# The end of a hybrid block written in another order, with shorter inverse roots and rare transfers on another queue

## Chip, cores and metric

One core of a Trainium2 chip runs the whole program. The metric is the time of one execution on the device in microseconds, less is better; the time given is the median of the runs. Beside it there is one profiled execution, whose trace all times of single instructions come from.

## The reference

512 tokens of 1024 features go through two layers, all in float32.

```python
def first_block(x, ...):
    h = rms_norm(x, norm_mix_w)
    z, xbc, dt_raw, q, k, v, f_raw = split(h @ w_in)
    y_ssd = ssd_mixer(...)          # chunked scan, group norm
    y_fox = fox_mixer(...)          # attention with forget gates, norms of q and k per head
    x = x + concat(y_ssd, y_fox) @ w_out
    return x + conv_gated_mlp(rms_norm(x, norm_ffn_w), ...)

def second_block(x, p, ...):
    h = rms_norm_2(x, mix_norm_g)
    y_r = (silu(rg) * head_group_norm(retention_chunkwise(...))) @ w_ret_o
    y_s = sliding_window_gqa(...) @ w_swa_o
    x = x + (sigmoid(gate_r) * y_r + sigmoid(gate_s) * y_s) @ w_out
    x = x + hierarchical_moe(rms_norm_2(x, ffn_norm_g), ...)   # 32 experts, two for each token
    ple = rms_norm_2(p @ w_ple, ple_norm_g)
    return x + sigmoid(rms_norm_2(x, ple_gate_norm_g) @ w_ple_gate) * ple
```

Each norm holds `lax.rsqrt(mean(x * x) + eps)`.

## The kernel before, in words

Tokens lie in four blocks of 128 (`NT = 4`); a product that has to be as exact as float32 is made of three matmuls of high and low halves (`mm3`, L251 to L253), whose halves ScalarE (L205, high) and VectorE (L208, low) make.

**Inverse roots.** No engine instruction gives the root itself: `rsqrt` computes it on VectorE from a shifted integer as first guess and three Newton steps, ten rows of 128 x 1, or thirteen where several columns are done at once (L326 to L343). It is called 43 times, in the norms of both mixers, of the feed-forward parts and of the gate. Outside the experts the order on each engine is found by a scheduler from its own costs, so that fewer rows in one place can change the order of others.

**The experts.** Of 256 slots for four experts each (64 a piece), one-hot matmuls gather the tokens. Experts are worked off in pairs, e = 0, 2, ... 30, by the class `Pair`: it asks SyncE's queue for eight chunks of `wgu` and four of `wdn`, 512 KB each, into a ring of chunk tiles `wc`; `up` makes 32 matmuls (L1116) and the gated value `hid` (L1119, L1120); `turn` transposes it into `hT` (L354, L1128); `down` makes 16 matmuls (L1136) and copies the two sums into the row tile `ye` (L1138 on ScalarE, L1139 on VectorE). A pair up to e = 28 is scattered to the buffer `ydram` by an indirect transfer of GpSimd (L1531). After e = 28, eight indirect transfers of GpSimd (L1773) gather, for each token block, its rows of the two chosen experts into `hf` tiles. The last pair (e = 30) doesn't go that way: `turned` (at e = 28) builds its one-hots `ohw` with VectorE (L1541, L1542), TensorE transposes them, and VectorE makes the 0/1 matrix `late` and the slots' weights `wslot` from them (L1545 to L1547); in the tail the last rows, weighted and split in high and low halves (L1564, L1565), are added to the tokens by matmuls with `late` (`pair`, L1573).

**The tail** is the gate. For each block t, `gathered` adds the gathered rows to x[t] (L1583 on VectorE, or L1580 on ScalarE with L1581 on GpSimd), `end` adds the sum of the last pair (L1589), `turn` transposes and splits x[t], and `logits` multiplies it with the gate's weights, 24 matmuls for 512 columns. The weights come in eight chunks, four for each half of the columns; `split` makes their high halves on ScalarE (L1818) and their low ones on VectorE (L1819). `eat` (L1835 to L1838) does the sigmoid, the product with `ple`, the sum with x and the output transfer. The order of the calls in `tail` is written by hand and is the order of the rows on TensorE, ScalarE, VectorE and GpSimd.

**The overflow.** Behind the tail stands a loop that takes care of experts with over 64 tokens (`overflow`). It goes round zero times with these inputs, but its instructions are in every engine's program.

Of the kernel before, what the change touches and what calls it, by code (L numbers as in the profile page):

```python
# [19 lines left out]
T = 512  # L20
# [152 lines left out]
class Chip:  # L173
# [146 lines left out]
    def rsqrt(self, ss, scale, tag="rs", pool=None, more=None):  # L320
# [24 lines left out]

    def row(self, key, pool, tag="row", t=None):
# [3 lines left out]
        self.nc.sync.dma_start(t, self.a["rows"][:, o:o + n].to_broadcast([128, n]))  # L350
        return t
# [743 lines left out]
class Pair:  # L1095
# [4 lines left out]
    def __init__(self, c, p, rows, chunks, wgu, wdn):  # L1100
        self.c, self.p, self.n = c, p, len(wgu)
        fetch = lambda ws, i: [chunks.fetch(w[:, i * 1024:i * 1024 + 1024]) for w in ws]
# [26 lines left out]

    def down(self):  # L1130
        c, r = self.c, 64 * self.n
        ps = [c.acc() for _ in range(2)]
        for j in range(2):
            for n in range(2):
                for i in range(self.n):
                    c.nc.tensor.matmul(ps[n][self.half(i)], self.hT[:, j, self.half(i)],  # L1136
                                       self.wd[j][i][:, n * 512:n * 512 + 512], start=j == 0, stop=j == 1)
# [5 lines left out]
def overflow(c, x, routing, slot, wt, extra, pled, out):  # L1143

    tc, nc, a = c.tc, c.nc, c.a
    v, s, pe = nc.vector, nc.scalar, nc.tensor
# [5 lines left out]
    with tc.For_i(0, some, 1):  # L1152
# [5 lines left out]
        w = c.row("n_ffn2", p)  # L1158
# [10 lines left out]
        for t in range(NT):  # L1169
            nc.sync.dma_start(ple[:, t], pled[t])  # L1170
# [5 lines left out]
        for n in range(2):  # L1176
            w = [gate_weights(c, c.fetch(a["wpleg"][n][:, i * 1024:i * 1024 + 1024]), i) for i in range(4)]
            for t in range(NT):
# [4 lines left out]
                gated(c, g, ps, r[t], x[t][:, ns], ple[:, t, ns], out[t * 128:t * 128 + 128, ns])  # L1183
# [4 lines left out]
def more_rounds(c, p, ring, x, hf, rel, wt, iota, wgu, wdn, rounds):  # L1188
# [5 lines left out]
    with tc.For_i(0, rounds * N_EXP * SLOTS, N_EXP * SLOTS) as r:  # L1194
        with tc.For_i(0, N_EXP, 1) as e:
# [23 lines left out]
            ex = Pair(c, p, p, chunks, [wgu[rows]], [wdn[rows]])  # L1219
# [229 lines left out]
def experts(c, x, routing, xtp, pled, out):  # L1449
# [84 lines left out]
    def turned(oT, w):  # L1534

        s4 = slots4(7)
        sums = p.tile([128, NT], F32, name="wsum")
        for t in range(NT):
            o = [p.tile([128, 128], F32, name=c.name("ohw"), tag=tag, bufs=1) for tag in ("ohw", "ohw2")]
            for k in range(2):  # L1540
                v.tensor_scalar(o[k], iota[:, 128:], s4[:, k, t:t + 1], wt[:, k, t:t + 1], op0=OP.is_equal, op1=OP.mult)  # L1541
            v.tensor_tensor(o[0], o[0], o[1], op=OP.add)  # L1542
            ps = c.aux()
            c.transpose(ps[:, :128], o[0])
            v.tensor_scalar(oT[:, t * 128:t * 128 + 128], ps[:, :128], 0.0, None, op0=OP.is_gt)  # L1545
            v.tensor_reduce(sums[:, t:t + 1], ps[:, :128], axis=AX.X, op=OP.add)
        v.tensor_reduce(w, sums, axis=AX.X, op=OP.add)  # L1547

    def tail():

        y = last.rows
        xt = BlockTiles(c, moe)
        junk = op.tile([128, D], F32, name="junk", tag="ohq", bufs=1)
        raws, w, pairs, r = [], [], {}, {}

        def fetch(i):
            raws.append(chunks.fetch(a["wpleg"][i // 4][:, i % 4 * 1024:i % 4 * 1024 + 1024], nc.sync if i < 4 else nc.scalar))

        def split(i):
            w.append(gate_weights(c, raws[i], i, [chunks.tile(F32R) for _ in "hl"]))  # L1560

        def half(n):
            ns = slice(n * 512, n * 512 + 512)
            s.activation(yh[:, ns], y[:, ns], AF.Copy, scale=ws)  # L1564
            v.scalar_tensor_tensor(yl[:, ns], y[:, ns], ws, yh[:, ns].bitcast(F32), op0=OP.mult, op1=OP.subtract)  # L1565

        def pair(t):

            pairs[t] = []
            for n in range(2):  # L1570
                ps = c.aux()
# [4 lines left out]
        def gathered(t, k, on_pool):  # L1576

            yk, wk = yg[t][:, k], first[:, k, t:t + 1]
            if on_pool:
                s.activation(yk, yk, AF.Copy, scale=wk)  # L1580
                nc.gpsimd.tensor_tensor(x[t], x[t], yk, op=OP.add)  # L1581
            else:
                v.scalar_tensor_tensor(x[t], yk, wk, x[t], op0=OP.mult, op1=OP.add)  # L1583
# [9 lines left out]

        def squares(ts):
            ss = c.sm([128, len(ts)], tag="gss")
            for i, t in enumerate(ts):
                s.activation(junk, x[t], AF.Square, accum_out=ss[:, i:i + 1])
            rs = c.rsqrt(ss, 1.0 / D, "gr")
            r.update({t: rs[:, i:i + 1] for i, t in enumerate(ts)})

        def logits(t, n, between=lambda: None):
            ps = c.aux() if n else c.acc()
            gate(c, ps, xt(t), w[4 * n:4 * n + 4], between)
            return ps

        def eat(ps, t, o, n=512, eng=None):
# [302 lines left out]
```

## Time and profile before

| | |
|---|---|
| median of 3 runs | 1619.01 us (1618.94 to 1623.02) |
| profiled execution | 1617.72 us, its span 1616.0 us |
| TensorE busy | 1517.5 us (94%) |
| VectorE busy | 923.9 us (57%) |
| ScalarE busy | 667.4 us (41%) |
| GpSimd busy | 135.2 us (8%) |
| moved | 246.64 MB, 153 GB/s over the span |

The span is the time from the first to the last instruction in the trace; what lies around it (1.7 us) belongs to the execution's time. In the rows, PE is TensorE, PEld its weight loads, DVE VectorE, ACT ScalarE, POOL GpSimd, SP SyncE; a q behind the name is that engine's queue of transfers. L12 is line 12 of the kernel before.

### The profile page before, as it was taken

What the parts mean: (1) busy time and instruction counts of PE and PEld (TensorE: products, weight loads), DVE (VectorE), ACT (ScalarE), POOL (GpSimd) and SP (SyncE); (2) the same over time, 40 slices, a digit from 0 to 9 for tenths busy, and PEclk for the clock granted to TensorE, in tenths of its full rate; (3) what the DMA queues carried; (4) which work ended last, traced back from release to release, by engine and by line L of the source; (5) the groups of instructions that cost most, each with busy time, mean ns of one, the idle gap of its engine ahead of it and who ended that gap; (6) DMA issues with size and microseconds to landing.
All of it is one profiled execution on the core that took longest, in us unless ns stands there. A gap on an engine that the chain in (4) does not pass through costs nothing.

```text
span 1616.0 us, 24407 instructions
## 1 busy us (share of the span) xinstructions
PE 1517.5 (94%) x9603; PEld 1256.3 (78%) x9603; DVE 923.9 (57%) x2122; ACT 667.4 (41%) x1107; POOL 135.2 (8%) x114
## 2 busy tenths in 40 slices
PE   3998989999999999999999998899999999999867
PEld 3776888999899988998889997887889855545356
DVE  4368688888864765436544524877644552232274
ACT  3364637656742544224432323369622421111143
POOL 3043310000000000000000001200000010000142
PEclk9999999999999999999999999999999999999979
DMA  9242212222250533233323522221213889999951
GB/s 320 90 156 92 79 61 71 79 92 68 90 159 25 183 92 97 75 116 97 96 72 102 192 83 91 105 75 58 91 64 125 302 330 411 409 410 409 383 199 55
DMA packets 75946, 246.64 MB, mean 153 GB/s; under 512 B 9486, under 2 KB 18446, under 8 KB 75456
## 3 DMA queue, kind: packets, MB, share of 16 engines
q1 hardware_dynamic: 69152, 220.80, 38.9%
q0 software_dynamic: 4944, 17.91, 3.0%
q10 hardware_dynamic: 1728, 6.29, 1.0%
q8 instruction: 78, 1.28, 0.3%
q14 instruction: 44, 0.36, 0.1%
HBM read 234.86 MB, written 24.18 MB: 160 GB/s over the span
## 4 chain that ended last, share of the span: by engine, by line
PE 73%; DVE 14%; ACT 6%; issue 3%; DMA 2%; POOL 1%; SPq 0%; ACTq 0%; POOLq 0%; DVEq 0%
PE acc L251 17%; PE acc L252 17%; PE acc L253 17%; PE acc L1116 6%; PE acc L1136 3%; PE aux L1476 3%; PE aux L354 3%; DVE wl L208 2%; PE aux L634 1%; ACT wh L205 1%; DMA wr<-in_wz_dram 1%; DVE de L554 1%; ACT pb L611 1%; DVE xn L362 1%; DVE rst L338 1%
## 5 line engine op out<-in xcount | busy, mean ns | idle before, releaser
L208 DVE TENSOR_TENSOR wl<-wr,wh 128x1024 fp32r<-128x1024 f32 (+1 forms) x177 | 213.6, 1209 | 253.5 <-ACT wh L205 248.6
L205 ACT ACTIVATE wh<-wr 128x1024 fp32r<-128x1024 f32 (+1 forms) x181 | 188.6, 1046 | 319.7 <-PE acc L253 158.9
L252 PE MATMUL acc<-xtl,wh 128*128 128x512 f32 (+2 forms) x744 | 278.6, 375 | 0.0
L251 PE MATMUL acc<-xth,wh 128*128 128x512 f32 (+2 forms) x744 | 277.3, 373 | 1.3 <-ACT wh L205 1.2
L253 PE MATMUL acc<-xth,wl 128*128 128x512 f32 (+2 forms) x744 | 277.0, 372 | 0.0
L251 PE MATMUL acc<-wh,xth 128*128 128x256 f32 x912 | 257.8, 284 | 3.8 <-ACT xth L205 2.0
L253 PE MATMUL acc<-wh,xtl 128*128 128x256 f32 x912 | 258.4, 284 | 0.8 <-DVE xtl L208 0.8
L252 PE MATMUL acc<-wl,xth 128*128 128x256 f32 x912 | 257.3, 283 | 1.2 <-DVE wl L208 1.1
L251 PEld LDWEIGHTS acc<-wh,xth 128*128 128x128 f32 x912 | 172.8, 190 | 7.5 <-ACT z L415 3.6
L252 PEld LDWEIGHTS acc<-wl,xth 128*128 128x128 f32 x912 | 173.0, 190 | 2.5 <-DVE wl L208 1.8
L253 PEld LDWEIGHTS acc<-wh,xtl 128*128 128x128 f32 x912 | 172.8, 190 | 1.6 <-DVE xtl L208 1.0
L251 PEld LDWEIGHTS acc<-xth,wh 128*128 128x128 f32 (+1 forms) x744 | 139.4, 187 | 27.1 <-ACT wh L205 1.9
L253 PEld LDWEIGHTS acc<-xth,wl 128*128 128x128 f32 (+1 forms) x744 | 139.3, 187 | 25.1 <-issue 0.5
L252 PEld LDWEIGHTS acc<-xtl,wh 128*128 128x128 f32 (+1 forms) x744 | 139.3, 187 | 24.3 <-issue 0.5
L1116 PE MATMUL acc<-wc,xg 128*64 128x512 f32 x512 | 112.6, 592 | 0.0
L251 PE MATMUL acc<-wh,acth 128*128 128x256 f32 x352 | 98.7, 280 | 0.1
L253 PE MATMUL acc<-wh,actl 128*128 128x256 f32 x352 | 98.3, 280 | 0.0
L252 PE MATMUL acc<-wl,acth 128*128 128x256 f32 x352 | 98.2, 279 | 0.0
L1116 PEld LDWEIGHTS acc<-wc,xg 128*64 128x64 f32 x512 | 36.7, 137 | 72.8 <-issue 64.3
L251 PEld LDWEIGHTS acc<-wh,acth 128*128 128x128 f32 x352 | 66.5, 189 | 0.6 <-ACT acth L205 0.5
L773 DVE SCALAR_TENSOR_TENSOR fcv<-acc,cols,fcv 128x511 f32<-128x511 f32 x88 | 65.7, 747 | 1.6
L252 PEld LDWEIGHTS acc<-wl,acth 128*128 128x128 f32 x352 | 66.5, 189 | 0.1
(476 smaller groups left out, 2618.2 us busy)
## 6 DMA issues: line engine op xcount, KB each, us to landing
wc<-in_wgu_dram SPq DMA_DIRECT2D x128, 512.0 KB, 10.7
wc<-in_wdn_dram SPq DMA_DIRECT2D x64, 512.0 KB, 10.8
wr<-in_wup_dram SPq DMA_DIRECT2D x44, 512.0 KB, 3.6
wr<-in_w2a_dram SPq DMA_DIRECT2D x28, 512.0 KB, 3.6
wr<-in_wqkv_dram SPq DMA_DIRECT2D x24, 512.0 KB, 3.7
wr<-in_wout_dram SPq DMA_DIRECT2D x24, 512.0 KB, 3.8
wr<-in_wdown_dram SPq DMA_DIRECT2D x16, 512.0 KB, 3.5
ydram<-in_x_dram POOLq DMA_DIRECT2D x15, 512.0 KB, 9.9
```

Source lines behind the costliest of these rows:

```text
L205: nc.scalar.activation(hi, src, AF.Copy)
L208: (nc.vector if engines[1] == "v" else nc.gpsimd).tensor_tensor(lo, src, hi.bitcast(F32), op=OP.subtract)
L251: mm(out, a[0], b[0], start=start, stop=False)
L252: mm(out, a[0], b[1], start=False, stop=False)
L253: mm(out, a[1], b[0], start=False, stop=stop)
L338: v.scalar_tensor_tensor(t, y, y, ms, op0=OP.mult, op1=OP.mult)
L354: self.nc.tensor.transpose(out, src, self.ident[:rows, :rows])
L362: nc.vector.scalar_tensor_tensor(out, xt_, r, wrow, op0=OP.mult, op1=OP.mult)
L773: v.scalar_tensor_tensor(y[:, sh:], ps[:, :T - sh], cv(k), y[:, sh:], op0=OP.mult, op1=OP.add)
L1116: c.nc.tensor.matmul(ps[self.half(i)], xg(kb, i), self.wu[kb // 2][i][:, kb % 2 * 512:kb % 2 * 512 + 512], start=kb == 0, stop=kb == KB - 1)
L1136: c.nc.tensor.matmul(ps[n][self.half(i)], self.hT[:, j, self.half(i)], self.wd[j][i][:, n * 512:n * 512 + 512], start=j == 0, stop=j == 1)
L1476: pe.matmul(ps[:, j], hf[t][:, k, ks], oq[:, t], start=start and k == 0, stop=stop and k == 1)
```

## The change

It has four parts, and line numbers move.

- `rsqrt`: a first guess that takes the shift into the multiplication, and two steps instead of three, seven rows for one column and nine for several.
- The last pair's one-hots: `weighted` builds them for all blocks at e = 24, `turned` transposes them in one PSUM tile behind pair 28's down product, one row each for `late` and `wslot`.
- The tail in another order. The first four gate chunks are asked for when the last pair's own chunks are; the last pair's sums are read in PSUM (no copy into `ye`); all of `gathered` is on VectorE; the high and low halves of the weights are separate calls; block 0's product isn't interrupted by block 1's transposes; the products with `ple` are on VectorE.
- The overflow loop's transfers are asked for by GpSimd rather than SyncE.

Line numbers: L354 is L355, L1116 is L1117, L1136 is L1137, L1545 and L1546 are L1558 and L1559, L1565 is L1587, L1573 is L1595, L1583 is L1600, L1589 is L1606, L1819 is L1580 in the tail.

```diff
@@ rsqrt
-        v.tensor_scalar(t.bitcast(I32), ms.bitcast(I32), 1, None, op0=OP.logical_shift_right)
-        v.tensor_scalar(y.bitcast(I32), t.bitcast(I32), -1.0, float(0x5F3759DF), op0=OP.mult, op1=OP.add)
-        for k in (1.0, -2.0, 16.0):
+        v.tensor_scalar(y.bitcast(I32), ms.bitcast(I32), -0.5, -553040512.0, op0=OP.mult, op1=OP.add)
+        for step in range(2):
...
-            v.scalar_tensor_tensor(y, t, -3.0 * k * k, y, op0=OP.add, op1=OP.mult)
-        v.tensor_scalar(y, y, -1.0 / 8192, None, op0=OP.mult)
+            if step == 0:
+                v.scalar_tensor_tensor(t, t, -2.0539012, t, op0=OP.add, op1=OP.mult)
+            v.scalar_tensor_tensor(y, t, -1.8898816 if step else 1.8970146, y, op0=OP.add, op1=OP.mult)
@@ overflow
+    queue = nc.gpsimd
...
-            nc.sync.dma_start(xi, routing.xd[t * 128:t * 128 + 128])
+            queue.dma_start(xi, routing.xd[t * 128:t * 128 + 128])
@@ last one-hots
+    def weighted():
         s4 = slots4(7)
+        ow, o2 = (p.tile([128, n, 128], F32, name=name) for name, n in (("ohw", NT), ("ohw2", 1)))
         for t in range(NT):
+            for k, o in enumerate((ow[:, t], o2[:, 0])):
+                v.tensor_scalar(o, iota[:, 128:], s4[:, k, t:t + 1], wt[:, k, t:t + 1], op0=OP.is_equal, op1=OP.mult)
+            v.tensor_tensor(ow[:, t], ow[:, t], o2[:, 0], op=OP.add)
+        return ow
+    def turned(ow, oT, w):
+        ps = c.aux()
+        for t in range(NT):
+            c.transpose(ps[:, t * 128:t * 128 + 128], ow[:, t])
+        v.tensor_scalar(oT, ps, 0.0, None, op0=OP.is_gt)
+        v.tensor_reduce(w, ps, axis=AX.X, op=OP.add)
@@ tail
+        last.turn()
+        high(0)
+        low(0)
+        rows = last.products(True)
+        half(0, rows[0])
+        gathered(0, 0)
+        half(1, rows[1])
+        gathered(0, 1)
+        high(1)
+        pair(0)
+        pair(1)
+        end(0)
+        turn(0)
+        pair(2)
+        low(1)
+        for i in (2, 3):
+            high(i)
+            low(i)
+        ps = {0: logits(0, 0)}
+        block(1)
+        pair(3)
...
+        ps[1] = logits(1, 0, (6,), lambda: block(2))
+        ss = [squares((0, 1))]
+        ps[2] = logits(2, 0, (4,), lambda: block(3))
@@ loop over the pairs
+            if e + 2 == N_EXP:
+                raws = [fetch_gate(i) for i in range(4)]
...
+            if e == 24:
+                ow = weighted()
             if e < COMBINED:
                 last.turn()
...
+            if e == 28:
+                turned(ow, late[:, :T], ws)
```

`block(t)` is `gathered` twice, `end` and `turn`; `(6,)` and `(4,)` are the feature blocks of the eight ahead of which it is called.

**TensorE at pair 28.** The first fence is the order before, from the last matmul of the pair's up product to the down product (`wc` are the chunks, `ohw` the one-hots):

```order
L1116 MATMUL acc_14583<-wc_14572,xg_14351 64x512
L354 MATMUL aux_14615<-cst,ohw_14610 128x128
L354 MATMUL aux_14624<-cst,ohw_14619 128x128
L354 MATMUL aux_14633<-cst,ohw_14628 128x128
L354 MATMUL aux_14642<-cst,ohw_14637 128x128
L354 MATMUL aux_14647<-cst,hid_14600 128x128 x2
L1136 MATMUL acc_14652<-wc_14574,hT_14650 64x512
L1136 MATMUL acc_14652<-wc_14576,hT_14650 64x512
```

The second is the order after, the same place up to pair 30's up product:

```order
L1117 MATMUL acc_14461<-wc_14450,xg_14213 64x512
L355 MATMUL aux_14485<-cst,hid_14478 128x128 x2
L1137 MATMUL acc_14490<-wc_14452,hT_14488 64x512
...
L1137 MATMUL acc_14491<-wc_14458,hT_14488 64x512
L355 MATMUL aux_14505<-cst,ohw 128x128 x4
L1117 MATMUL acc_14573<-wc_14540,xg_14213 64x512
```

The one-hots' four transposes stood ahead of the transposes of `hid` and the down product; they now stand behind the down product, in one row.

**VectorE in the tail.** Before, from the first addition of a gathered row (`hf`) to x0 on; `wc` with `cols` is a row pair that makes the low half of a weight chunk:

```order
L1583 SCALAR_TENSOR_TENSOR x_1814_12069<-hf_14667,first,x_1814_12069 128x1024
L1819 SCALAR_TENSOR_TENSOR wc_14787<-wc_14746,cols,wc_14786 128x512 x2
L1583 SCALAR_TENSOR_TENSOR x_1814_12069<-hf_14667,first,x_1814_12069 128x1024
L1589 TENSOR_TENSOR x_1814_12069<-x_1814_12069,aux_14779 128x512
L1589 TENSOR_TENSOR x_1814_12069<-x_1814_12069,aux_14782 128x512
L1819 SCALAR_TENSOR_TENSOR wc_14798<-wc_14748,cols,wc_14797 128x512 x2
L208 TENSOR_TENSOR hf_14811<-aux_14812,hf_14811 128x512
L208 TENSOR_TENSOR hf_14811<-aux_14819,hf_14811 128x512
L1819 SCALAR_TENSOR_TENSOR wc_14827<-wc_14750,cols,wc_14826 128x512 x2
L1583 SCALAR_TENSOR_TENSOR x_1815_12070<-hf_14668,first,x_1815_12070 128x1024
L1589 TENSOR_TENSOR x_1815_12070<-x_1815_12070,aux_14805 128x512
```

After, from the low half of the first weight chunk on:

```order
L1580 SCALAR_TENSOR_TENSOR wc_14598<-wc_14565,cols,wc_14597 128x512 x2
L1587 SCALAR_TENSOR_TENSOR wc_14483<-acc_14614,wslot,wc_14482 128x512
L1600 SCALAR_TENSOR_TENSOR x_1814_11941<-hf_14512,first,x_1814_11941 128x1024
L1587 SCALAR_TENSOR_TENSOR wc_14483<-acc_14615,wslot,wc_14482 128x512
L1600 SCALAR_TENSOR_TENSOR x_1814_11941<-hf_14512,first,x_1814_11941 128x1024
L1606 TENSOR_TENSOR x_1814_11941<-x_1814_11941,aux_14632 128x512
L1606 TENSOR_TENSOR x_1814_11941<-x_1814_11941,aux_14635 128x512
L208 TENSOR_TENSOR hf_14646<-aux_14647,hf_14646 128x512
L208 TENSOR_TENSOR hf_14646<-aux_14654,hf_14646 128x512
L1580 SCALAR_TENSOR_TENSOR wc_14600<-wc_14567,cols,wc_14599 128x512 x2
L1580 SCALAR_TENSOR_TENSOR wc_14602<-wc_14569,cols,wc_14601 128x512 x2
L1580 SCALAR_TENSOR_TENSOR wc_14604<-wc_14571,cols,wc_14603 128x512 x2
```

Before, the weights' low halves stand between the additions, and x1 gets one addition on this queue, the rest on GpSimd; after, three weight chunks stand between x0's split and x1, whose two additions are both here.

**ScalarE at the end of the first mixer.** Before, with the exponentials `ssde` and `de` and the gate `z`:

```order
L551 ACT_TABLE_LOAD
L551 ACTIVATE ssde_1686<-ssde_1686 128x24
L415 ACT_TABLE_LOAD
L415 ACTIVATE z_1358<-acc_1384 128x256
L415 ACTIVATE z_1358<-acc_1486 128x256
L415 ACTIVATE z_1358<-acc_1485 128x256
...
L360 ACTIVATE yn_1661,nss_1662<-y_1657 128x512
L555 ACT_TABLE_LOAD
L555 ACTIVATE de_1691<-de_1691 128x1024
```

After, in the same place:

```order
L556 ACT_TABLE_LOAD
L556 ACTIVATE de_1600<-de_1600 128x1024
L416 ACT_TABLE_LOAD
L416 ACTIVATE z_1334<-acc_1461 128x256
L573 ACTIVATE st_1591<-aux_1589 128x512
L552 ACT_TABLE_LOAD
L552 ACTIVATE ssde_1659<-ssde_1659 128x24
L416 ACT_TABLE_LOAD
L416 ACTIVATE z_1334<-acc_1360 128x256
...
L556 ACT_TABLE_LOAD
L556 ACTIVATE de_1664<-de_1664 128x1024
L205 ACTIVATE wh_1854<-wr_1852 128x1024
L416 ACT_TABLE_LOAD
L416 ACTIVATE z_1334<-acc_1462 128x256
```

The rows are the same, in another order, and each change between kinds of function brings a table load: the stage has 23 of them before and 27 after.

## Rows read from the trace of the kernel before

**Rows 1.** Windows: us, PE, PEld, DVE, ACT, POOL busy, granted clock, DMA share, GB/s

```profile
...
0.00:250.00 250.00, 205.04 (x1296) 174.98 (x1297) 162.05 (x387) 118.24 (x173) 69.23 (x64) 0.99 0.40 130
1311.00:1500.00 189.00, 189.00 (x1056) 95.05 (x1056) 50.61 (x119) 23.69 (x52) 15.38 (x16) 1.00 1.03 407
...
1545.00:1562.00 17.00, 9.93 (x29) 7.13 (x28) 15.50 (x11) 7.58 (x12) 11.07 (x5) 0.50 0.71 258
1562.00:1608.00 46.00, 44.99 (x226) 37.48 (x224) 24.89 (x54) 17.82 (x30) 9.58 (x7) 1.00 0.14 52
```

**Rows 2.** Timeline of TensorE: start, us, what, [idle before, releaser]

```profile
...
1510.68 1.46 PE L1116 MATMUL acc<-wc,xg 128*64 128x512 f32 x6
...
1516.77 0.30 PE L354 MATMUL aux<-cst,ohw 128*128 128x128 f32 x1 [1.85 <-DVE ohw L1542]
...
1517.98 5.12 PE L1136 MATMUL acc<-wc,hT 128*64 128x512 f32 x16 [0.69 <-DVE wslot L1547]
1522.93 7.03 PE L1116 MATMUL acc<-wc,xg 128*64 128x512 f32 x32
...
1531.91 3.65 PE L1136 MATMUL acc<-wc,hT 128*64 128x512 f32 x16 [0.56 <-issue]
...
1544.01 1.97 PE L354 MATMUL aux<-cst,x 128*128 128x128 f32 x8 [4.69 <-DVE x L1589]
...
1558.86 1.94 PE L354 MATMUL aux<-cst,x 128*128 128x128 f32 x8 [4.77 <-DVE x L1589]
```

**Rows 3.** Waits of TensorE, 0 to 1100 us: us in total, times, longest

```profile
...
PE aux L354 <- DVE ryn L887: 9.8, 4, 4.8
...
PE aux L354 <- DVE yn L362: 6.4, 6, 1.9
```

**Rows 4.** Timeline of the end, SyncE's last transfer

```profile
...
1608.44 0.33 SPq L1838 DMA_DIRECT2D out_dram<-g  x1
```

**Rows 5.** Timeline of SyncE's queue, the last experts' chunks

```profile
...
1516.91 4.15 SPq L1091 DMA_DIRECT2D wc<-in_wdn_dram  x4
```

**Rows 6.** DMA issues, 1510 to 1566 us: KB each, median us to landing

```profile
...
wc<-in_wdn_dram SPq DMA_DIRECT2D x4, 512.0 KB, 10.3
...
hf<-ydram,sloti POOLq DMA_INDIRECT x8, 6.8
```

**Rows 7.** Timeline of GpSimd, last scatter to additions

```profile
...
1524.59 0.96 POOL L1531 DMA_INDIRECT ydram<-ye,rowi  x1 [16.85 <-DVE ye L1139]
1532.12 1.06 POOL L1773 DMA_INDIRECT hf<-ydram,sloti  x1 [6.57 <-PE aux L354]
...
1549.00 7.90 POOL L1581 TENSOR_TENSOR x<-x,hf 128x1024 f32<-128x1024 f32 x3 [0.76 <-ACT hf L1580]
```

**Rows 8.** DMA issues, 1311 to 1500 us, the scatters

```profile
...
ydram<-ye,rowi POOLq DMA_INDIRECT x13, 7.2
```

**Rows 9.** Timeline of VectorE, 1540 to 1558 us

```profile
...
1540.55 1.41 DVE L1819 SCALAR_TENSOR_TENSOR wc<-wc,cols,wc 128x512 fp32r<-128x512 f32 x2
1541.88 1.28 DVE L1583 SCALAR_TENSOR_TENSOR x<-hf,first,x 128x1024 f32<-128x1024 f32 x1
1543.26 1.29 DVE L1589 TENSOR_TENSOR x<-x,aux 128x512 f32<-128x512 f32 x2
1544.47 4.33 DVE L1819 SCALAR_TENSOR_TENSOR wc<-wc,cols,wc 128x512 fp32r<-128x512 f32 x2
...
1549.92 4.79 DVE L1819 SCALAR_TENSOR_TENSOR wc<-wc,cols,wc 128x512 fp32r<-128x512 f32 x2
1554.63 3.35 DVE L1583 SCALAR_TENSOR_TENSOR x<-hf,first,x 128x1024 f32<-128x1024 f32 x1
```

**Rows 10.** Timeline of VectorE, first and last of a call's 13 rows

```profile
...
1034.78 0.17 DVE L326 TENSOR_SCALAR grm<-gn 128x4 f32<-128x4 f32 x1
...
1037.21 0.17 DVE L343 TENSOR_SCALAR gry<-gry 128x4 f32<-128x4 f32 x1
```

**Rows 11.** Groups of ScalarE, 0 to 250 us, largest of table loads

```profile
...
L498 ACT ACT_TABLE_LOAD x9 | 11.5, 1283 | 1.6 <-DVE cv L493 1.3 <-DVE rsy L334 0.2
```

More of the change, by code (lines that the diff above doesn't have):

```diff
@@ L1095, with __init__ @@
 class Pair:
-    def __init__(self, c, p, rows, chunks, wgu, wdn):
+    def __init__(self, c, p, rows, chunks, wgu, wdn, queue=None):
         self.c, self.p, self.n = c, p, len(wgu)
-        fetch = lambda ws, i: [chunks.fetch(w[:, i * 1024:i * 1024 + 1024]) for w in ws]
+        fetch = lambda ws, i: [chunks.fetch(w[:, i * 1024:i * 1024 + 1024], queue) for w in ws]
         self.wu = [fetch(wgu, i) for i in range(4)]
@@ L1128, in turn, with products @@
         c.nc.vector.tensor_copy(self.hT, pt[:, :2 * r].rearrange("p (j n) -> p j n", j=2))
+    def products(self, halves=False):
+        c = self.c
+        ps = [c.acc() for _ in range(2)]
+        for j, n in sorted(((j, n) for j in range(2) for n in range(2)), key=lambda jn: jn[::-1] if halves else jn):
+            for i in range(self.n):
+                c.nc.tensor.matmul(ps[n][self.half(i)], self.hT[:, j, self.half(i)],
+                                   self.wd[j][i][:, n * 512:n * 512 + 512], start=j == 0, stop=j == 1)
+        return ps
     def down(self):
         c, r = self.c, 64 * self.n
[L1132 to L1137, printed above, removed]
+        ps = self.products()
         c.nc.scalar.activation(self.rows[:, :512], ps[0][:r], AF.Copy)
@@ L1176, in overflow @@
         for n in range(2):
-            w = [gate_weights(c, c.fetch(a["wpleg"][n][:, i * 1024:i * 1024 + 1024]), i) for i in range(4)]
+            w = [gate_weights(c, c.fetch(a["wpleg"][n][:, i * 1024:i * 1024 + 1024], queue), i) for i in range(4)]
             for t in range(NT):
@@ L1218, in more_rounds @@
             rows = bass.ds(e * 128, 128)
-            ex = Pair(c, p, p, chunks, [wgu[rows]], [wdn[rows]])
+            ex = Pair(c, p, p, chunks, [wgu[rows]], [wdn[rows]], nc.gpsimd)
             ex.up(lambda kb, i: xg[:, kb])
@@ L1549, in tail, with fetch_gate @@
+    def turned(ow, oT, w):
[4 more added lines that the diff above has]
+        v.tensor_reduce(w, ps, axis=AX.X, op=OP.add)
+    def fetch_gate(i, queue=None):
+        return chunks.fetch(a["wpleg"][i // 4][:, i % 4 * 1024:i % 4 * 1024 + 1024], queue)
     def tail():
-        y = last.rows
         xt = BlockTiles(c, moe)
         junk = op.tile([128, D], F32, name="junk", tag="ohq", bufs=1)
-        raws, w, pairs, r = [], [], {}, {}
@@ L1556, in fetch, with high @@
[L1556 to L1562, printed above, removed]
+        w, pairs, r = {i: [chunks.tile(F32R) for _ in "hl"] for i in range(4)}, {}, {}
+        def high(i):
+            if i not in w:
+                w[i] = [chunks.tile(F32R) for _ in "hl"]
+            for j in range(2):
+                o = slice(j * 512, j * 512 + 512)
+                s.activation(w[i][0][:, o], raws[i][:, o], AF.Copy, scale=c.col("n_pleg", i % 4 * 2 + j))
@@ L1592, in turn, with block @@
             c.to_xt(x[t], xt(t))
+        def block(t):
+            for k in range(2):
+                gathered(t, k)
+            end(t)
+            turn(t)
         def squares(ts):
@@ L1820, in gate_weights, with gate @@
     return h, l
-def gate(c, ps, xb, w, between=lambda: None, o=0, n=512):
+def gate(c, ps, xb, w, between=lambda: None, at=(), o=0, n=512):
     for kb in range(KB):
-        if kb == KB // 2:
+        if kb in at:
             between()
@@ L1829, in gate, with gated @@
         c.mm3(ps, (xb[0][:, kb], xb[1][:, kb]), (wk[0][:, ns], wk[1][:, ns]), kb == 0, kb == KB - 1)
-def gated(c, g, ps, r, x, ple, out, eng=None):
+def gated(c, g, ps, r, x, ple, out, eng=None, queue=None):
     nc = c.nc
```

105 lines of the change are left out of this document (35 added, 70 removed).

## The prediction

> **What bounds the kernel now.** I read the busy time and granted clock by stretch first, then TensorE's idle time at the two ends, then VectorE, GpSimd and the transfers of the last 100 us. From 1311 to 1500 us TensorE has matmul work all of the time while the weights stream at 407 GB/s; nothing that the change does reaches that stretch [rows 1]. Time can come or go in three places. First, the last experts and the gate: between 1545 and 1562 TensorE is busy 9.93 of 17 us at a granted clock of 0.50 (the lower level, 1.2 GHz), and from 1562 on it is busy 44.99 of 46 us at 1.00 [rows 1]. So the gate's end is fixed by the moment from which TensorE is never short of work again. That moment is the transposes of token block 1 at 1558.86, ahead of which it idled 4.77 us for VectorE's last addition to x1 [rows 2]. Second, the short dependent rows of the inverse roots in the early stages, behind which TensorE waits at some ten places [rows 3]. Third, what runs after the last output transfer is asked for at 1608.44: the span is 1616.0, so 7.6 us [rows 4].
>
> **One-hots sooner.** TensorE ends the up product of pair 28 at 1512.1, then waits for VectorE's one-hots up to 1.85 us at a time, and begins that pair's down product only at 1517.98; it runs 5.12 us where the next pair's equal one takes 3.65 [rows 2]. The next pair shows the way without one-hots: up ends 1529.96, down starts 1531.91, 1.95 us later. With the four transposes put behind it, the down product should start at about 1514.1 and end at 1517.9, 5.2 us sooner than 1523.1. But what follows is held by transfers: the last chunk of wdn of pair 30 is asked for at about 1520.7 [rows 5] and lands 10.3 us later by the median [rows 6], at 1531.0 or a little after. The last four matmuls of the last down product need it, some 1 us, so that ends at about 1532.5 rather than 1535.56. Of 5.2 us only 3.0 arrive there. The asking sooner of the gate's first four chunks I cost at nothing: on SyncE's queue they stood directly behind wdn of pair 30, and still do.
>
> The scatter gains more. GpSimd asked for it at 1524.59, 1.5 us behind the down product, and for the first gather at 1532.12, behind the scatter's landing [rows 7]. Now: scatter asked for at 1519.4, landed after 7.2 us (the median of 13 inside the saturated stream [rows 8]) at 1526.6, first gather asked for 0.8 later at 1527.4. Alone, gathers landed after 6.8 us [rows 6] and were asked for 1.37 apart: 1534.2 and 1535.6 for the two of x0. They now share the engines with the last chunks, so I take 1534.6 and 1537.1. x0 then has its second addition at 1538.4 (1.28), the last pair's part at 1539.7 (1.29 for two halves) [rows 9], and its transposes, allowing for the last pair's own products, start at about 1540.5 against 1544.01 [rows 2]. The copy of the last down product into ye falls away and its sum is read in place; that lies inside the 1540.5.
>
> **Additions on VectorE alone.** Five additions leave GpSimd (three of them took 7.90 us [rows 7]) and cost VectorE 1.28 each: 6.4 us more. But beside them VectorE's own work was stretched: pairs of rows that took 1.41 took 4.33 and 4.79, and an addition 3.35 instead of 1.28 [rows 9]. That is 2.9 + 3.4 + 2.1 = 8.4 us given back. The order counts more than these 2 us. From x0's transposes VectorE now has, in its queue: two rows of x0's split (to 1543.2, ScalarE's half between), the low halves of three weight chunks at 1.41 (to 1547.5), two additions to x1 (to 1550.1), and the last pair's part, 0.65 a half. Block 1's transposes start when the first half is there, 1550.9, 8.0 us before 1558.86. Block 0's first gate product fits in ahead: 24 matmuls from 1542.3, 5.6 us at the full clock, 10.2 at the lower.
>
> From block 1's transposes to the last output's issue it was 1608.44 - 1558.86 = 49.6 us. In that time TensorE did 12 matmuls of block 0 that now lie ahead (226 rows in 45 us, 48 of them half as wide, so 0.22 each, 2.7 us) and one more set of the last pair's products than now (0.9). That leaves 46.0. Two things cancel: eight transposes took 1.94 us at the lower clock there (about 1 at the full one), and block 3's additions now stand behind block 2's split in VectorE's queue, a stall of some 1 us. 1550.9 + 46.0 = 1596.9: **the tail gives 11.5 us**. Bounds: 8 (block 0's product at the lower clock until 1552.5, two such stalls) and 14 (gathers unshared).
>
> **Short inverse roots.** A call of 13 rows took 2.6 us, so 0.2 each [rows 10]; three (one column) or four rows go. Where TensorE waits behind such a chain (four times for the retention's norm, six for the first mixer's [rows 3]) that is 0.6 to 0.8 us: at most 8 us in ten places. Elsewhere the rows lie beside full TensorE work; were that cover gone, the 146 rows taken away would be 29 us. Against it, shorter calls let the scheduler order the first mixer anew, and ScalarE has 27 table loads there instead of 23, 1.28 us each [rows 11]: 5.1 us on an engine busy 118 of 250 us [rows 1]. Covered, they cost nothing. Between these ends I take **3.5 us gained**, half the roots' 8 less a tenth of the loads; bounds a loss of 5 (no root shows, all loads do) and a gain of 8.
>
> **Rare transfers on GpSimd.** None of them runs here: the loop that holds them goes round zero times. What can change is how long a queue takes to pass it: SyncE has 35 rows fewer, GpSimd 33 more. Of the 7.6 us I take **1.5 gained**, between 0 (another queue passes as slowly) and 3. The Trainium skill, Runtime: NRT & Kernel Launch, section Instruction fetch mechanics, says that a taken branch to a place outside the two pages at hand forces a fetch before the engine goes on. By it, GpSimd's longer body would still cost that fetch, and the term would be 0; no row here shows which engine is last.
>
> **Sum.** The profiled execution took 1617.72 us. 1617.72 - 11.5 - 3.5 - 1.5 = 1601.2. The median of the three runs, 1619.01, lies 1.3 above it, so the forecast is 1602.5.
>
> **Rivals.**
> *The clock stays low (0.18).* TensorE still pauses some 2 us between the last pair's products and x0's transposes, and then works in pieces behind VectorE's weight rows. If 0.50 holds until 1562 as before, block 0's product ends at 1552.5 (1.6 later) and the 9.5 us from there do half their work (4.8 lost): the tail gives 5.1, and 1608.9 comes out. For it: the stretch to 1562 shows 0.50 throughout though TensorE worked 9.93 of 17 us. Against it: that work had a 4.77 us gap in it, where now it would run on.
> *The early stages lose (0.12).* The new order and four loads cost 5 us instead of 3.5 gained: 1611.
> *They gain more (0.10).* All ten places give 0.8 us, the loads are covered, the new order gives 1.5 more: 1596.5.
> *Moving the one-hots gives nothing (0.04).* The early gathers and the last weight chunks take from each other: gathers at half the speed, the fourth chunk of the gate 8 us late, so that the split behind it waits as x1 did before. The tail keeps 2 us, the early stages lose 2: 1617.5, no change. The Trainium skill, DMA: Bandwidth & Descriptors, section Queues, rings and completion order, has each transfer engine go round its queue rows packet by packet; by that, both sides would have half while both last. Against so large a price: 7.2 us for a scatter inside the saturated stream [rows 8] and 6.8 for a gather after it [rows 6].
> *Slower (0.03).* VectorE takes its rows in order, so a late gather of x0 now stops the low halves behind it, and TensorE with them. My chain has 13.8 us from x0's second gather to block 1's transposes. If that gather lands at 1553.6 instead of 1537.1, all 16.5 us are gone; at 1560 the time would be 1619.0 + 6.4 = 1625. Asked for at 1528.8, its transfer would have to take 25 to 31 us, four times what gathers took.
>
> **Chances and range.** Forecast 0.53 (1598 to 1606). What a measurement here can tell from no change is about 0.3%, 4.9 us: below 1614.1 lie the forecast and the first three rivals, 0.93; same 0.04, slower 0.03. For 8 in 10 the range goes from 1594 (the larger early gain, tail bound) to 1610 (the low clock).
>
> **What would show it.** Right: pair 28's down product starts some 4 us sooner, the first gather is asked for 4 to 5 us sooner, GpSimd adds nothing, the weight rows take 1.41 a pair throughout, block 1's transposes start 8 us sooner against the expert stream's start, and that stream itself starts 3.5 sooner. Wrong: block 1's transposes less than 4 us sooner, a granted clock of 0.50 that lasts past them, an expert stream that starts later, or 7.6 us still behind the last issue.

## The result and the profile after

The changed kernel took 1603.16 us at the median of four runs (1600.57 to 1607.67), the kernel before 1620.3 at the median of four; the ratio is 0.9891, with a 95% interval of 0.9871 to 0.9910. So 1.1% faster. The profiled execution took 1600.57 us with a span of 1598.8, 17.2 less than before's.

Three points cut that span: the end of pair 28's up product, the last output's issue, and the end. TensorE's timeline of the changed kernel:

```profile
...
1498.70 7.10 PE L1117 MATMUL acc<-wc,xg 128*64 128x512 f32 x32
...
1507.68 3.83 PE L1137 MATMUL acc<-wc,hT 128*64 128x512 f32 x16 [0.52 <-DVE hT L1129]
...
1517.20 2.94 PE L1117 MATMUL acc<-wc,xg 128*64 128x512 f32 x8 [0.17 <-DMA wc<-in_wgu_dram]
...
1524.21 4.05 PE L1137 MATMUL acc<-wc,hT 128*64 128x512 f32 x16 [0.56 <-issue]
1529.90 0.50 PE L1595 MATMUL aux<-wc,wc 128*128 128x512 f32 x1 [1.63 <-ACT wc L1575]
...
1534.98 1.91 PE L355 MATMUL aux<-cst,x 128*128 128x128 f32 x8
...
1545.60 1.23 PE L355 MATMUL aux<-cst,x 128*128 128x128 f32 x8 [1.34 <-DVE x L1606]
```

Pair 28's up product ends at 1505.80; before it was 1512.13 [rows 2], so the early stages gave 6.3 us. The last output, in the timeline of the end, was asked for 17.2 us sooner than before [rows 4]:

```profile
...
1591.28 0.33 SPq L1861 DMA_DIRECT2D out_dram<-g  x1
```

So the tail, from the end of pair 28's up product to the last issue, took 85.5 us instead of 96.3: 10.8 gained. Behind the last issue 7.5 us remain, as before: nothing. Forecast were 3.5, 11.5 and 1.5.

In the tail GpSimd asks for the first gather 14.9 us behind the up product instead of 20.0 [rows 7], as its timeline shows:

```profile
...
1520.68 1.06 POOL L1796 DMA_INDIRECT hf<-ydram,sloti  x1 [6.73 <-DMA ydram<-ye,rowi]
```

Block 1's transposes start 39.8 us behind the up product rather than 46.7, and from there to the last issue it is 45.7 us (forecast 46.0). VectorE's timeline shows the gate's three low halves in one piece at 0.68 a row, right ahead of x1's additions:

```profile
...
1528.69 1.42 DVE L1580 SCALAR_TENSOR_TENSOR wc<-wc,cols,wc 128x512 fp32r<-128x512 f32 x2 [4.58 <-DMA wc<-in_wpleg_dram]
...
1538.16 4.05 DVE L1580 SCALAR_TENSOR_TENSOR wc<-wc,cols,wc 128x512 fp32r<-128x512 f32 x6
1542.14 2.60 DVE L1600 SCALAR_TENSOR_TENSOR x<-hf,first,x 128x1024 f32<-128x1024 f32 x2
1544.77 1.28 DVE L1606 TENSOR_TENSOR x<-x,aux 128x512 f32<-128x512 f32 x2
```

The windows of the same kernel (columns as in [rows 1]) show a granted clock of 0.50 from 1534 to 1538 and 0.92 in the next 4 us, where before it was 0.50 for all of 1545 to 1562 [rows 1]:

```profile
...
1534.00:1538.00 4.00, 4.00 (x15) 3.27 (x15) 2.34 (x4) 1.67 (x3) 0.00 (x0) 0.50 0.39 156
1538.00:1542.00 4.00, 4.00 (x17) 3.25 (x16) 4.00 (x7) 1.97 (x4) 0.00 (x0) 0.92 0.03 12
...
1560.00:1590.00 30.00, 29.83 (x152) 24.96 (x150) 18.53 (x43) 13.18 (x22) 0.00 (x0) 1.00 0.17 66
```

### The profile page after: what moved, and what is told of

Read it like the earlier page. It is cut to its first block, busy times and chain, and to the rows that moved or that the text cites. A ratio compares the mean times of both kernels' runs of the same rounds, so it can differ in the third digit from the quotient of the medians.

```text
span 1598.8 us, 24250 instructions
## 1 busy us (share of the span) xinstructions
PE 1517.5 (95%) x9603; PEld 1254.7 (78%) x9603; DVE 898.8 (56%) x1980; ACT 663.1 (41%) x1103; POOL 111.2 (7%) x102
## 4 chain that ended last, share of the span: by engine, by line
PE 74%; DVE 12%; ACT 6%; DMA 5%; issue 2%; POOL 0%; SPq 0%; ACTq 0%; DVEq 0%; POOLq 0%
PE acc L252 18%; PE acc L251 18%; PE acc L253 18%; PE acc L1117 5%; PE aux L355 3%; PE aux L1485 3%; PE acc L1137 3%; DMA wc<-in_wgu_dram 2%; DVE wl L208 1%; PE aux L635 1%; ACT wh L205 1%; DMA wr<-in_wz_dram 1%; PE aux L522 1%; DMA wc<-in_wpleg_dram 1%; DMA wc<-in_wdn_dram 1%
## 5 line engine op out<-in xcount | busy, mean ns | idle before, releaser
L1117 PE MATMUL acc<-wc,xg 128*64 128x512 f32 x512 | 115.5, 593 | 0.4 <-DMA wc<-in_wgu_dram 0.4
L1117 PEld LDWEIGHTS acc<-wc,xg 128*64 128x64 f32 x512 | 37.4, 137 | 74.9 <-issue 63.3
```

Source lines behind the costliest of these rows:

```text
L1117: c.nc.tensor.matmul(ps[self.half(i)], xg(kb, i), self.wu[kb // 2][i][:, kb % 2 * 512:kb % 2 * 512 + 512], start=kb == 0, stop=kb == KB - 1)
```

## The experiments

Each kernel below was timed against the kernel before on the same chip, 4 to 12 executions of each; the ratio is to that kernel, with its 95% interval. Where single microseconds are told apart, they are read in the one profiled execution between the three points above, since whole executions of one kernel differ by more (the changed kernel's four by 7.1 us).

In the six profiled executions with the changed tail as it stands (the changed kernel and experiments 2, 3, 4, 8 and 10), the tail took 85.5 to 86.8 us; differences of 1 us there say nothing. Block 1's transposes came 38.8 to 39.8 us behind the up product, and from there to the last issue it was 45.7 us in two of the six and 47.2 to 47.3 in four. In those four TensorE's granted clock was 0.58 to 0.69 in the 4 us from these transposes on, in the two it was 1.00.

**1. The inverse roots alone.** The kernel before with the new `rsqrt`, nothing else.

> The kernel before with the short inverse roots alone. Theory (the parts add up, and the roots give 6.4 us of the 17, nearly all of it in the retention between 990 and 1100 us, nothing net in the first 265 us): the expert stream starts 6.4 us sooner, the span is about 1609.6, the tail from pair 28 on as before. Rival 1 (the forecast's own term): 3.5 us, spread over ten places, span 1612.5, the stream 3.5 sooner. Rival 2 (the early gain came from elsewhere, the order that the other parts bring): the stream less than 2 us sooner.

Ratio 0.9966 (0.9952 to 0.9980), 1615.88 us. The tail stayed at 96.1 us. TensorE's 1400th row (about 265 us) came 2.2 us later than before, its 7000th (about 1110) 4.4 sooner: 6.3 us gained between 967 and 1110 us, none ahead of it. Up to pair 28 only 1.3 us were left in that execution, as the first mixer and the stretch from 1110 to 1283 lost; by the medians the roots are worth 0.3%, some 5.5 us. So the theory holds for the place, and the ten even places don't; its size, 6.4, fits the medians and not that execution, where a stream 1.3 us sooner is the sign of rival 2.

**2. The end alone.** The changed kernel with the long `rsqrt` and `queue = nc.sync`.

> The changed kernel with the long inverse roots and the rare transfers back on SyncE, so the sooner one-hots and the new order of the tail alone. Theory: the stream starts where it did before, within 0.3 us; from there to the last output's issue it takes 10.9 us less; span about 1605.2. Rival (the tail's gain needs the earlier start, because the weight stream ran ahead there): 7 us less, span 1609.

Ratio 0.9923 (0.9908 to 0.9938), 1608.29 us. The up product ended 1.1 us later than before, the tail took 85.5 us: 10.8 gained, to the tenth what the whole change showed. The parts add, also by the ratios (0.34% and 0.77%, together 1.09%).

**3 and 4. The overflow loop left out, and its transfers back on SyncE.**

```diff
-    overflow(c, x, routing, slot, wt, extra, pled, out)      # 3
-    queue = nc.gpsimd                                        # 4
+    queue = nc.sync
...
-            ex = Pair(c, p, p, chunks, [wgu[rows]], [wdn[rows]], nc.gpsimd)
+            ex = Pair(c, p, p, chunks, [wgu[rows]], [wdn[rows]], nc.sync)
```

> The changed kernel without the overflow loop, which goes round zero times with these inputs; it leaves out that loop's code alone. Measures what is left of the 7.5 us behind the last output's issue. Theory (some queue's passing of the loop takes 3 us, whichever holds the transfers): 4.5 us or less behind the last issue, span about 1595.8. Rival (the 7.5 us are the transfer's landing and the program's own end, and passing the loop costs nothing): 7.5 us again, span 1598.8. If the third possibility holds, that loading the loop's instructions takes transfer time elsewhere, the difference lies ahead of the last issue.

> The changed kernel with the rare transfers back on SyncE. Theory (another engine passes the loop as late as SyncE did): 7.5 us behind the last issue, span 1598.8 within 0.3. Rival (the forecast's term): 1.5 us more behind the last issue, span 1600.3.

With the loop left out the ratio was 0.9874 (0.9855 to 0.9892), 1601.67 us, and its timeline ends so, with a span of 1602.4:

```profile
...
1599.15 0.33 SPq L1860 DMA_DIRECT2D out_dram<-g  x1
```

3.2 us lie behind the last issue, not 7.5: passing the loop of no rounds, with the loading of the two counts that decide on its rounds, costs 4.3 us there. (Ahead of it this execution was later, by 8.7 us in the first mixer alone, see below.) Whether all of the 4.3 us reach the whole time is not shown: the intervals of the kernels with and without the loop overlap. With the transfers back on SyncE the ratio was 0.9887 (0.9872 to 0.9903), 1602.79 us, and again 7.5 us lay behind. Which queue holds the transfers doesn't matter.

**5. The one-hots alone.** The kernel before with `weighted` at e = 24 and `turned` behind pair 28's down product.

> The kernel before with the last one-hots built at e = 24 and transposed behind pair 28's down product; nothing else. Theory: that down product starts about 4 us sooner after its up product, the first gather is asked for 4 to 6 us sooner, and the last output's issue comes 3 to 4 us sooner counted from pair 28's up product, since x0 was waiting for its gathers; VectorE's rows beside GpSimd's additions stay stretched. Rival 1 (all of the tail's 10.9 us come from the order of VectorE's queue, the gathers were no limit): less than 1 us. Rival 2 (all of it from the one-hots): 8 us or more.

Ratio 0.9976 (0.9964 to 0.9989), 1618.41 us. The down product started 1.9 us behind its up product and not 5.9; the first gather was asked for 5.5 us sooner; the tail took 95.8 us, 0.5 less. For the tail of this execution rival 1 holds. The whole executions say something else: their median is 3.9 us below that of the kernel before (1.8 to 5.8 by the interval), which would fit the theory. The one trace doesn't show where, and the profile of before that it is held against is a short execution (1617.72 us, below all 16 of that kernel timed here). So the worth of the one-hots alone stays open between 0.5 and some 4 us. VectorE's weight rows, in its timeline, were stretched as ever:

```profile
...
1545.74 4.23 DVE L1825 SCALAR_TENSOR_TENSOR wc<-wc,cols,wc 128x512 fp32r<-128x512 f32 x2
...
1551.09 4.70 DVE L1825 SCALAR_TENSOR_TENSOR wc<-wc,cols,wc 128x512 fp32r<-128x512 f32 x2
```

**6. The one-hots late, in the changed kernel.** `turned` with its building put back ahead of pair 28's down product.

> The changed kernel with the last one-hots built and transposed where the kernel before has them, ahead of pair 28's down product. Theory after the run of the one-hots alone (they gave 0.5 us there, since the old order of VectorE's queue was the limit): in the new order x0's additions come early enough to wait for the gathers, so here late one-hots cost 2 to 4 us from pair 28's up product to the last output's issue; the first gather is asked for 5 us later. Rival 1 (they are worth as little as alone): under 1 us. Rival 2 (the early gathers delay the gate's first chunk, so late ones help): the last issue sooner than in the changed kernel.

Ratio 0.9895 (0.9872 to 0.9918), 1603.42 us, beside 0.9891 for the changed kernel; the tail took 86.0 us, inside the spread. My expectation of 2 to 4 us failed, rival 1 holds. TensorE's and VectorE's timelines:

```profile
...
1513.20 5.11 PE L1137 MATMUL acc<-wc,hT 128*64 128x512 f32 x16 [0.69 <-DVE wslot L1556]
...
1537.00 1.97 PE L355 MATMUL aux<-cst,x 128*128 128x128 f32 x8 [0.55 <-DVE x L1603]
...
1547.68 1.23 PE L355 MATMUL aux<-cst,x 128*128 128x128 f32 x8 [1.62 <-DVE x L1603]
```

```profile
...
1528.94 1.42 DVE L1577 SCALAR_TENSOR_TENSOR wc<-wc,cols,wc 128x512 fp32r<-128x512 f32 x2 [1.93 <-DMA wc<-in_wpleg_dram]
...
1533.01 1.28 DVE L1597 SCALAR_TENSOR_TENSOR x<-hf,first,x 128x1024 f32<-128x1024 f32 x1 [1.99 <-DMA hf<-ydram,sloti]
```

In the kernel before VectorE's first weight row was this one:

```profile
...
1533.59 1.42 DVE L1819 SCALAR_TENSOR_TENSOR wc<-wc,cols,wc 128x512 fp32r<-128x512 f32 x2 [1.78 <-ACT wc L1818]
```

x0 now does wait for its gathers, and its transposes come 29.6 us behind the up product instead of 29.2 (28.1 to 29.3 in the six executions), those of block 1 40.3 instead of 39.8 (38.8 to 39.8). But the gate's first chunk is there sooner: its low half starts 21.6 us behind the up product as before (21.5), against 22.9 in the changed kernel. Of these 1.4 us 0.3 is that the chunk was asked for later; from then to ScalarE's first row on it, 10.8 us passed in the four profiled kernels with late one-hots and 11.8 to 12.1 in eight with early ones. What the early gathers gain they take in part from the weights.

**7. Five additions on GpSimd, in the changed kernel.** As in the kernel before: ScalarE scales, GpSimd adds the first gathered row of x1 and both of x2 and x3.

```diff
+        def added(t, k):
+            s.activation(yg[t][:, k], yg[t][:, k], AF.Copy, scale=first[:, k, t:t + 1])
+            nc.gpsimd.tensor_tensor(x[t], x[t], yg[t][:, k], op=OP.add)
...
         gathered(0, 1)
+        added(1, 0)
...
         pair(2)
+        for t in (2, 3):
+            for k in range(2):
+                added(t, k)
```

> The changed kernel with five of the eight gathered additions back on GpSimd (ScalarE scales the rows first): the first of x1, both of x2 and x3, as in the kernel before; the rest of the new order stays. Theory (VectorE's two-operand rows stand still beside GpSimd's additions): the six rows of the three weight chunks, 4.05 us in the changed kernel, take 7 us or more, block 1's transposes come 1 to 4 us later from pair 28's up product, and the last output's issue 1 to 4 us later. Rival (VectorE's queue is the bound, five rows fewer help): block 1's transposes 1 us sooner or more, the last issue too.

Ratio 0.9931 (0.9913 to 0.9949), 1610.17 us. The tail took 93.0 us, 7.5 more than in the changed kernel and 6.2 more than the longest of the six. Timelines of GpSimd and VectorE:

```profile
...
1540.10 10.95 POOL L1605 TENSOR_TENSOR x<-x,hf 128x1024 f32<-128x1024 f32 x4 [0.85 <-ACT hf L1604]
```

```profile
...
1539.74 3.55 DVE L1580 SCALAR_TENSOR_TENSOR wc<-wc,cols,wc 128x512 fp32r<-128x512 f32 x2
1544.03 8.22 DVE L1580 SCALAR_TENSOR_TENSOR wc<-wc,cols,wc 128x512 fp32r<-128x512 f32 x4 [0.75 <-ACT wc L1575]
```

While GpSimd adds, the six weight rows take 11.8 us instead of 4.05; another 0.75 us is VectorE's wait for ScalarE, which scales gathered rows first. Block 1's transposes come 47.3 us behind the up product, as late as in the kernel before (46.7). The theory holds, at a higher price than expected: the additions stand here in one lump beside all three chunks.

**8 and 9. The product of ple with its norm's weight on VectorE**, in the changed kernel and in the kernel before.

```diff
-        nc.gpsimd.tensor_tensor(o, o, w, op=OP.mult)
+        v.tensor_tensor(o, o, w, op=OP.mult)
```

> The changed kernel with the product of the ple rows with their norm weight (L1830, 128 x 1024, four times, beside the retention's norms) on VectorE instead of GpSimd. Theory (in 990 to 1050 us single small VectorE rows stood 2.3 to 2.6 us behind that product; the short roots gained there by meeting it less often): no root row over 0.3 us is left, TensorE's waits for the retention's norm fall from 2.1 and 3.9 to 1 to 2 us each, and the stretch from 967 to the 1100s is 2 to 4 us shorter. Rival (the rows are late for another reason, or VectorE's four more rows of 1.3 us cost as much): within 1 us of the changed kernel there.

> The kernel before with the product of the ple rows with their norm weight on VectorE instead of GpSimd; long inverse roots. Theory (what the short roots gained in the retention was meeting GpSimd's product twice rather than four times): no root row over 0.3 us there, TensorE's waits for the retention's norm fall from 9.8 us to 1 to 3, and the stretch between 967 and 1110 us is 7 to 11 us shorter, more than the short roots alone gave (5.5). Rival (the short roots gained by their own length, 0.8 us a call): the stretch is 0 to 3 us shorter.

These ask why the retention gave 5.5 us when its four calls are only 0.8 shorter each. GpSimd's and VectorE's timelines of the kernel before:

```profile
...
997.38 2.39 POOL L1807 TENSOR_TENSOR ple<-ple,n_ple 128x1024 f32<-128x1024 f32 x1 [69.50 <-ACT ple L1803]
1000.16 2.35 POOL L1807 TENSOR_TENSOR ple<-ple,n_ple 128x1024 f32<-128x1024 f32 x1 [0.39 <-ACT ple L1803]
...
1014.43 2.42 POOL L1807 TENSOR_TENSOR ple<-ple,n_ple 128x1024 f32<-128x1024 f32 x1
1019.41 2.65 POOL L1807 TENSOR_TENSOR ple<-ple,n_ple 128x1024 f32<-128x1024 f32 x1 [2.56 <-ACT ple L1803]
```

```profile
...
997.53 2.28 DVE L326 TENSOR_SCALAR grm<-gn 128x4 f32<-128x4 f32 x1
...
1000.25 2.29 DVE L340 TENSOR_TENSOR grt<-gry 128x4 f32<-128x4 f32 x1
...
1014.16 2.72 DVE L334 TENSOR_SCALAR gry<-grt 128x4 int32<-128x4 int32 x1
...
1019.78 2.31 DVE L343 TENSOR_SCALAR gry<-gry 128x4 f32<-128x4 f32 x1
```

Rows of 128 x 4 that take 0.17 us elsewhere took 2.3 to 2.7 beside GpSimd's product, with one SBUF operand or two, and each of the four ended 0.03 to 0.04 us behind the end of a product. The chain of 13 met it four times, that of 9 in the changed kernel twice. TensorE's wait for the norm was 9.8 us before [rows 3], and in the changed kernel:

```profile
...
PE aux L355 <- DVE ryn L888: 6.4, 3, 3.9
```

With the product on VectorE, in the changed kernel:

```profile
...
PE aux L355 <- DVE ryn L888: 0.5, 2, 0.3
```

There the ratio is 0.9854 (0.9832 to 0.9876), 1598.75 us; the stretch from 967 to 1110 us was 12.7 us shorter than before, the changed kernel's own 5.5, so the product gave 7.2 where I had expected 2 to 4. No root row over 0.3 us is left in this stretch of either kernel, which shows that the long rows came from GpSimd's product. In the kernel before the waits for the norm went from 9.8 to 0.8 us, but 3.8 came back where VectorE makes `sv`:

```profile
...
PE acc L251 <- DVE sv L208: 3.8, 1, 3.8
PE aux L354 <- DVE ryn L887: 0.8, 2, 0.5
```

Ratio 0.9970 (0.9955 to 0.9985), 1616.39 us; the stretch was 6.1 us shorter, less than the 7 to 11 that I had expected and no more than the short roots alone gave (6.3). So the theory that the short roots gained by meeting the product less often fails: where no row meets it any more, they still make the stretch 6.6 us shorter (12.7 less 6.1). The rival, 0 to 3 us by their own length, fails too. The two gains add, and why the short roots give about twice the 3.2 us of the retention's own rows stays open. (The four calls for the norm of ple lie in this stretch too, three rows shorter each; I had not counted them.)

The clock adds to each wait, as windows of before and of the changed kernel show:

```profile
...
1000.00:1010.00 10.00, 5.83 (x29) 5.05 (x28) 8.80 (x37) 4.41 (x11) 2.98 (x2) 0.83 0.13 53
...
1020.00:1030.00 10.00, 6.34 (x32) 6.34 (x33) 8.44 (x19) 1.80 (x5) 2.06 (x1) 0.66 0.48 157
```

```profile
...
1010.00:1020.00 10.00, 6.12 (x28) 5.58 (x28) 8.87 (x23) 5.44 (x13) 2.97 (x2) 0.66 0.32 107
```

Two stretches at 0.83 and 0.66 before, one at 0.66 after; with the product on VectorE in the changed kernel all of 990 to 1050 is at 1.00. Of the 12.7 us 9.4 are idle time of TensorE, and 3.3 are its own work: as many rows (804) kept it busy for 131.9 us before, at a mean granted clock of 0.96, and for 128.6 here, at 0.99.

**10. Long roots in the first norm and first mixer only.** A flag in `rsqrt`, changed behind `first_mixer`.

> The changed kernel with the long inverse roots inside the first norm and first mixer (the first 265 us) and the short ones after. Theory (the short roots' own gain there is given back by the new order: four more table loads, a longer wait near 147 us and the lower clock behind it): 23 table loads there, TensorE's place at 265 us between 1.5 us sooner and 0.5 later than in the changed kernel, so nothing is lost by the long roots. Rival (the short roots gained there, and chance took it): 2 to 5 us later.

Ratio 0.9875 (0.9857 to 0.9894), 1601.88 us. 23 table loads again, and the 1400th row 0.6 us sooner than in the changed kernel: the short roots give nothing there. Windows of the changed kernel, then of the kernel before, show a longer wait near 147 us and a lower clock behind it; that these take the gain back fits, but is not shown, and the kernel before has a low stretch of its own a little earlier (0.69 and 0.80 from 126 to 140 us):

```profile
...
146.00:152.00 6.00, 3.17 (x18) 3.20 (x19) 5.58 (x9) 1.88 (x2) 1.04 (x1) 0.79 0.42 154
152.00:160.00 8.00, 8.00 (x28) 6.00 (x28) 4.83 (x11) 0.50 (x2) 1.28 (x1) 0.73 0.00 0
```

```profile
...
146.00:152.00 6.00, 4.44 (x20) 3.30 (x18) 6.00 (x13) 0.81 (x2) 0.73 (x1) 1.00 0.32 102
152.00:160.00 8.00, 7.62 (x43) 6.42 (x44) 5.93 (x9) 1.72 (x3) 3.56 (x2) 1.00 0.32 111
```

Over the profiled executions the 1400th row came 0.5 to 8.7 us later than in before's with short roots there (seven, 1.8 in the middle), and 0.5 sooner to 1.8 later with long ones (six with before's own). That the new order is worse by more than chance is likely, not settled.

**11. A better version.** Experiments 8 and 10, and the last pair's halves ahead of the first gate chunk's:

```diff
-        high(0)
-        low(0)
         rows = last.products(True)
...
         gathered(0, 1)
+        high(0)
         high(1)
...
         end(0)
+        low(0)
         turn(0)
```

> The changed kernel with three edits: long inverse roots in the first norm and first mixer, the ple rows' product on VectorE, and in the tail the last pair's halves ahead of the first weight chunk's (so that they don't stand behind its transfer). Theory: the three add up, 0.5 to 2 us in the first mixer, 4 us from the retention, and 1 to 2 us in the tail, where TensorE's 1.3 us wait ahead of block 1's transposes goes; span 1592 to 1595, median 1595 to 1598. Rival (the tail's start is held by the gathers or by VectorE's queue in whatever order): nothing in the tail, span 1594 to 1597.

Ratio 0.9827 (0.9801 to 0.9853), 1592.48 us, the fastest median, though its interval overlaps that of experiment 8; the profiled span is 1591.0. Both are a little below what I had expected. Timelines of TensorE and VectorE:

```profile
...
1491.61 7.04 PE L1130 MATMUL acc<-wc,xg 128*64 128x512 f32 x32
...
1526.90 1.25 PE L368 MATMUL aux<-cst,x 128*128 128x128 f32 x8 [2.85 <-DVE x L1619]
...
1537.32 1.22 PE L368 MATMUL aux<-cst,x 128*128 128x128 f32 x8 [1.10 <-DVE x L1619]
```

```profile
...
1524.77 1.28 DVE L1613 SCALAR_TENSOR_TENSOR x<-hf,first,x 128x1024 f32<-128x1024 f32 x1 [2.20 <-DMA hf<-ydram,sloti]
```

The tail took 84.4 us, 1.1 below the fastest with the changed order, but that is no gain that can be told: block 1's transposes come 38.7 us behind the up product (38.8 to 39.8 in the six), TensorE's wait ahead of them is still 1.10 us, and x0's second addition now waits 2.20 us for its gather. So the rival's nothing in the tail can't be excluded. The stretch from 967 to 1110 was 14.0 us shorter than before, 8.5 more than in the changed kernel where I had expected 4. The first mixer gave nothing in this execution (1.8 later).

## Why the prediction was right, and where not

**The total** was right (1602.5 forecast, 1603.16 measured), and so was the weight of the tail. That the sum came so close is in part luck: the early stages gave 2.8 us more than their term, the tail 0.7 and the rare transfers 1.5 less.

**Tail, 11.5: 10.8 measured.** Block 1's transposes came 6.9 us sooner, not 8.0; the rest to the last issue was 45.7, not 46.0 (in four of the six executions 47.2 to 47.3). That the order of VectorE's queue and the additions decide was right, and experiment 7 shows how much: in the new order 7.5 us hang on GpSimd's additions, where I had netted 2.0 from the rows and left the rest to the order. What the rest of the new order gives by itself no run takes apart.

**One-hots: the step that failed inside the tail.** The down product started 4.0 us sooner, the first gather was asked for 5.1 sooner, as worked out. (My chain has the down product's end at 1517.9; 1514.1 and 3.65 make 1517.75, which changes nothing.) But that this makes x0's transposes 3.5 us sooner was wrong: they came 2.7 us sooner, and 2.2 of it also with late one-hots (experiment 6). Nor did the 3.0 us arrive at the last down product: pair 30's up product began 4.6 us sooner but took 10.3 us instead of 7.03, as it now came to its chunks of wgu early and waited for them, and its down product ended 1.0 us sooner. The first gate chunk, 1.4 us later (1.1 of it with the gathers beside it), stood ahead of the last pair's halves on ScalarE: TensorE waited 1.63 us for it at 1529.90. I had let half of each transfer go to the gathers and not asked what the other side lost; the rival that the two take from each other was right in kind, and its price was some 1 us, not 8. In the tails of the profiled executions the one-hots were worth 0.5 us in either kernel, no more than the spread; the 3.9 us of experiment 5's medians have no place yet.

**Inverse roots, 3.5: some 5.5 to 6.3.** The step that failed is the row price: 0.6 to 0.8 us at each of ten places. Six places, the first mixer's, gave nothing in sum; the order and the table loads changed as I had allowed for, but that these took the gain is not shown. The retention's stretch gave 5.5 to 7.3 us, and 6.6 with no contention left (experiments 8 and 9), so its price is about twice that of its rows, for a reason that stays open. Beside it lay a gain that I didn't see: root rows there were not 0.2 us but up to 2.7 beside GpSimd's product, worth 6.1 us with long roots and 7.2 with short ones. I had that contention in the tail [rows 9] and did not look for it where the waits of [rows 3] were up to 4.8 us, six times a call's saving. That no engine instruction gives the root, as the words on the kernel have it, is meant of this kernel; no run tried one.

**Rare transfers, 1.5: 0.0.** 7.5 us remained. The step that failed is that the queue of the transfers decides how long the loop takes to pass: experiment 4 shows no difference. The Trainium skill, Runtime: NRT & Kernel Launch, section Instruction fetch mechanics, says that a taken branch to a place outside the two pages at hand costs a fetch. By that the term was to be 0, and it was; experiment 3 shows a price, 4.3 us for this loop with the loading of its counts, and not that it is the fetch.

**The low clock** stayed a rival: 0.50 in 1534 to 1538, 0.92 in the next 4 us, in which TensorE worked 8.00 of 8 us; the 4.77 us gap of before is gone. In four of the six executions the clock fell once more, behind block 1's transposes, and the rest took 1.6 us more. Why it falls again in some executions and not in others no run shows.

## What to carry to other kernels

Before moving elementwise work to GpSimd to relieve VectorE, look at what VectorE's rows cost beside it: here five additions there saved VectorE 6.4 us of rows and cost the end 7.5, and a product of 2.4 us on GpSimd held tiny rows of VectorE for up to 2.7 us each. A chain of short rows is priced by the waits it sits in, not by its row count alone (5.5 to 7.3 us where the rows made 3.2). And a transfer made earlier inside a saturated stream takes its time from the one beside it: ask which of the two is needed first.

## What the runs showed of the hardware

- Rows of VectorE with 4 elements a partition and a single SBUF operand (L326, L334, L343) stood 2.3 to 2.7 us beside a GpSimd product of 2.4 to 2.7 us and ended 0.03 to 0.04 us behind its end. The Trainium skill, SBUF — State Buffer, section Who interferes with whom, counts on contention from two SBUF inputs or a two-port mode. Which of these rows ran in such a mode no view shows.
- A loop of no rounds at the program's end, with the loading of its two counts, cost 4.3 us behind the last issue (7.5 us with it, 3.2 without).
- Around TensorE's waits of 3.9 to 4.8 us in the retention, windows of 10 us show a granted clock of 0.66 to 0.83, so that a wait there costs more than its length. With the product on VectorE and the short roots the stretch fell by 12.7 us, of which 9.4 were idle time and 3.3 TensorE's own rows.
- A 512 KB weight chunk was usable 10.8 us after it was asked for, and 11.8 to 12.1 us where eight gathers started some 5 us sooner beside it.
